# Where the weight sums of a seven-product feed-forward layer are made: VectorE or accumulating transfers

## The chip, the cores and the metric

The kernel runs on one core of a Trainium2 chip. The metric is device time in microseconds (us) of one execution. The engines are TensorE (PE, with its weight loads as PEld), VectorE (DVE), ScalarE (ACT), GpSimd (POOL) and SyncE (SP), whose queue issues most DMAs. Each engine works through its instructions in the order of the program and waits on semaphores.

## The reference

Two layers of a hybrid decoder over 16 + 512 tokens of width 1024: a norm, an input projection, two groups of attention heads, an output projection, then the feed-forward part with which the change deals (inner width 2816), and at the end a norm.

```python
hn = rmsnorm(h, ffn_norm_g)
ff = silu(einsum('bld,df->blf', hn, w_gate)) * einsum('bld,df->blf', hn, w_up)
return h + einsum('blf,fd->bld', ff, w_down)
```

## The kernel before

**Numbers.** Every product of two float32 matrices is three passes of TensorE in a rounded format (fp32r): high part of the weight by high part of the activation, high by low, low by high. A weight block is loaded to a tile (`raw` or `fraw`), ACT casts it to the high part (`whi`, `fwhi`, line 941) and DVE subtracts to get the low part (`wlo`, `fwlo`, line 942); both lines are in `splits`. `whi` and `fwhi` are rings of a few buffers, which come free when PE has used them.

**The feed-forward part.** The 2816 inner columns are 22 blocks of 128. Blocks 0 and 1 go plainly (`dense_steps`). Blocks 2 to 21 are objects of the class `Unit`: gate and up of a block together are treated as a 2 x 2 matrix of blocks (rows: gate and up; columns: the lower and the upper four of the eight 128-row pieces of the 1024 inputs), the tokens and inputs as another, and seven products of blocks take the place of eight. With a0, a1 the halves of gate and b0, b1 those of up, the seven products need the weights

- w1 = (a0, a1), the gate block as loaded (`make1`);
- w2 = (b0 + b1 - a0, b0 + b1), two sums that DVE makes into a tile `S` (lines 1084 and 1085, `make2`);
- w3 = (a0 - b0, b1), with one sum, made over b0 in `fraw` (line 1092, `make3`);
- w4 = a1 - (b0 + b1 - a0), made over a1 in `raw` (line 1098, `make4`).

The matching sums of activations are made once a layer in `x_forms` (four calls, k = 0 to 3): DVE makes four forms into `S`, and ACT and DVE split them into the tiles `th` and `tl` (line 155 is in `split`). `head` does the products of w1, `middle` those of w2 and the first half of w3, `tail` the rest. The seven products go into three PSUM banks, x, y and z. Bank x is accumulated on further and further, and between two accumulations ACT copies it out to a tile `e` (`keep`, line 1117), because its value so far is needed too; PE's next products into the same bank wait for that copy. At the end `done` makes silu(gate) times up and splits it into `ah` and `al`, the activations of the down products.

**Order.** `ffn` builds a list of steps, each a chunk of matmuls, and runs them in turn. Weights are jobs: `need(j)` at the first chunk of a job loads and converts the next few jobs ahead, so that loads (SP) and casts (ACT, DVE) stand well ahead of their products. Units 2 and 3 do their heads first, and then each unit's middle and tail are mixed with products of a round of down weights (`ROUNDS`, lines 27 to 30), whose blocks of w_down come into `raw` too. `raw` has four buffers, `fraw` and `S` two. GpSimd does nothing in the feed-forward part.

Of the kernel before, what the change touches and what calls it, by code (L numbers as in the profile page):

```python
# [16 lines left out]
NK = D // 128  # L17
# [24 lines left out]
def hybrid_kernel(ctx, tc, x_t, w_in, w_fl, w_out, w_gate, w_up, w_down, vecs, b_fg, rope, decay, mask, ident, out_t):  # L42
# [107 lines left out]
    def vcol(c):  # L150
        return vec[:, c:c + 1]
# [137 lines left out]
    def fft(tag, dt=F32R, shape=(128, T), bufs=None):  # L289
        return phase["ffn"].tile(list(shape), dt, name=tag, tag=tag, bufs=bufs)  # L290
# [570 lines left out]
    def ffn(l, st, real, last):  # L861
# [43 lines left out]
        def x_forms(k):  # L905
            def go():
                if k == 0:
                    st["t"] = [[fft(f"t{p}{i}", shape=(128, 2, 4, w)) for p in "hl"] for i in range(2)]
                s = fft("S", F32, (128, 6, w), 2)
                a, b = ((h[k][:, c0:c1], h[HB + k][:, c0:c1]) for c0, c1 in HC)  # L910
                g0, g1 = vcol(V_FFN + l * NK + k), vcol(V_FFN + l * NK + HB + k)
                with tc.issue_after(st["scaled"].ins) if real else ExitStack():
                    nc.scalar.activation(s[:, 0:2], two(h[k]), AF.Copy, scale=g0)
                nc.vector.tensor_sub(s[:, 2], s[:, 1], s[:, 0])
                for i in range(2):
                    nc.vector.scalar_tensor_tensor(s[:, 3 + i], b[1], g1, s[:, 1 + i], ALU.mult, ALU.subtract)
                nc.vector.scalar_tensor_tensor(s[:, 5], a[1], g1, s[:, 4], ALU.mult, ALU.subtract)
# [74 lines left out]
        class Pair:  # L992
# [14 lines left out]

            def make1(self, hi, lo):
                r = self.t["r"]
                s = self.t["s"] = fft("S", F32, (128, HB, 128), 2)  # L1010
# [33 lines left out]
            def steps(self):  # L1044
# [7 lines left out]
                        product(self.w2, 4, b(1, 1), y, False, True, 2, self.add(0, None, "zy")),  # L1052
                        product(self.w2, 2, form(r, 4), x, False, True, 2, self.add(1, 0, "x")))

        class Unit:
            def __init__(self, f):
                self.f = f
# [9 lines left out]

            def load(self):
                if "a" not in self.t:
                    for n, src, pool, tag, bufs in (("a", w_gate, wp, "raw", 4), ("b", w_up, phase["ffn"], "fraw", 2)):  # L1070
                        self.t[n] = pool.tile([128, NK, 128], F32, name=tag, tag=tag, bufs=bufs)
                        nc.sync.dma_start(self.t[n], src[l, self.f])


            def make1(self, hi, lo):
# [2 lines left out]


            def make2(self, hi, lo):  # L1080
                a, b = self.t["a"], self.t["b"]
                s = self.t["s"] = fft("S", F32, (128, NK, 128), 2)
                with tc.high_priority() if self.f == PLAIN else ExitStack():
                    nc.vector.tensor_add(s[:, HB:NK], b[:, 0:HB], b[:, HB:NK])
                    nc.vector.tensor_sub(s[:, 0:HB], s[:, HB:NK], a[:, 0:HB])
                    splits(hi, lo, s)


            def make3(self, hi, lo):
                a, b = self.t["a"], self.t["b"]  # L1090
                with tc.high_priority(60) if self.f == PLAIN else ExitStack():
                    nc.vector.tensor_sub(b[:, 0:HB], a[:, 0:HB], b[:, 0:HB])
                    splits(hi, lo, b)


            def make4(self, hi, lo):
                a, s = self.t["a"], self.t["s"]
                nc.vector.tensor_sub(a[:, HB:NK], a[:, HB:NK], s[:, 0:HB])
                splits(hi, lo, a[:, HB:NK])

            def bank(self, n):
                def go():
# [24 lines left out]
            def done(self):  # L1127
                e = self.t["e"]
                sg = tt("sg")
                with tc.high_priority():  # L1130
                    nc.vector.tensor_add(two(sg), self.t["zy"][:, :, 0:w], e[:, 0:2])
                c = slice(t0, T)
                nc.vector.scalar_tensor_tensor(sg[:, c], sg[:, c], RSC, st["R"][:, c], ALU.mult, ALU.mult)
                silu(sg[:, c], None if self.f < NF - 1 else ROOTS if last else LOGS)
                u = tt("tq")
                nc.vector.scalar_tensor_tensor(u[:, c], sg[:, c], RSC, st["R"][:, c], ALU.mult, ALU.mult)
                u2 = two(u)
                nc.vector.tensor_mul(u2[:, 0], self.t["x"][:, 0:w], u2[:, 0])
                nc.vector.tensor_mul(u2[:, 1], e[:, 2], u2[:, 1])
# [74 lines left out]
        for r, (f0, f1) in enumerate(ROUNDS):  # L1214
            for f in range(f0, f1):
                if f < PLAIN:
                    if f == 0:
                        st["first"] = range(len(jobs), len(jobs) + 3)
                    steps += dense_steps(w_gate[l, f], [(0, xs, NK, QC, g_done(f) if f else held.append)], banks=f == 1, own=own, far=f == 1, after=st["after"][2 * f])
                    steps += dense_steps(w_up[l, f], [(0, xs, NK, QC, u_done(f))], own=None if f else own, far=f == 0, after=st["after"][1 + 2 * f])  # L1220
                    continue
                for i in (f, f + 1) if f == PLAIN else (f,):
                    if i not in units:
                        units[i] = Unit(i)
                        steps += units[i].head()
# [32 lines left out]
        else:  # L1258
# [46 lines left out]

            def square_b(m):
                if m == 0:
                    t = fft("S", F32, (128, 6, w), 2)
# [89 lines left out]
            def after_7():  # L1398
# [23 lines left out]
        return steps  # L1422

    gf = const.tile([128, NK], F32, name="gf")
    nc.vector.tensor_scalar_mul(gf, vec[:, V_FIN:V_FIN + NK], RSC)

# [200 lines left out]
```

## Time and profile before

| what | us |
|---|---|
| time, median of 3 runs | 1249.9 (1249.72 to 1250.13) |
| span of the profiled execution | 1248.2 |
| TensorE busy | 1236.6 (99%) |
| VectorE busy | 1062.2 (85%) |
| ScalarE busy | 733.5 (59%) |
| GpSimd busy | 294.6 (24%) |
| the two feed-forward parts, about | 270 to 655 and 890 to 1190 |

The profiled execution's time is its span of 1248.2 us, 1.7 us under the median of the runs. A row of a group of instructions reads: line, engine, operation, tiles written and read, shape, count, then busy us and mean ns of one, then the idle time of the engine just before them and what ended it. A row of a stretch reads: from and to, its length, then busy us of PE, PEld, DVE, ACT and POOL (with the number of instructions), the clock granted to TensorE, the mean share of the time in which the 16 DMA engines were busy, and GB/s. A row of a timeline reads: start, length, and the instruction, with the wait ahead of it in brackets. A DMA row ends with the size and the median us from issue to landing. Times up to about 655 are the first layer.

### The profile page before, as it was taken

The page shows a single profiled execution, that of the slowest core. Times are in us where ns is not written, and L with a number is a line of the kernel's source. Part 1 is how long each engine was busy: PE and PEld are TensorE (multiplying, and loading weights), DVE is VectorE, ACT ScalarE, POOL GpSimd, SP SyncE. Part 2 cuts the span into 40 slices and gives each one's busy share as a digit, 9 for nine tenths or more (in the row PEclk, how much of TensorE's full clock was granted, in tenths as well). Part 3 has the DMA queues.
Part 4 walks back from the last instruction along what each step waited for, and adds up shares of the span by engine and source line. Part 5 has one row for each costly group of instructions (what it writes and reads, how often), then busy time and mean ns, then how long its engine had stood idle before and what let it go on. Part 6 is the DMA issues. An engine that isn't in the chain of part 4 may idle for free.

```text
span 1248.2 us, 24164 instructions
## 1 busy us (share of the span) xinstructions
PE 1236.6 (99%) x9387; PEld 1192.1 (96%) x9387; DVE 1062.2 (85%) x2033; ACT 733.5 (59%) x1397; POOL 294.6 (24%) x568
## 2 busy tenths in 40 slices
PE   9999999999999999999999999999999999999997
PEld 9999999999999999999999989999799999999996
DVE  7887756889997999899876877568999989998996
ACT  7767655776544555455566766567765445454554
POOL 4555655440000000000035556554400000000000
PEclk9999999999999999999999999999999999999999
DMA  6222222222433233322312222231414333333322
GB/s 238 68 77 69 78 69 85 60 85 72 133 119 102 85 102 118 103 86 85 114 65 85 63 84 75 68 94 52 141 54 135 111 102 102 100 104 102 102 69 69
DMA packets 43347, 116.25 MB, mean 93 GB/s; under 512 B 5088, under 2 KB 9952, under 8 KB 43232
## 3 DMA queue, kind: packets, MB, share of 16 engines
q1 hardware_dynamic: 42800, 114.41, 28.8%
q8 instruction: 74, 1.21, 0.4%
q14 instruction: 41, 0.34, 0.1%
q10 hardware_dynamic: 432, 0.29, 0.1%
HBM read 112.58 MB, written 2.10 MB: 92 GB/s over the span
## 4 chain that ended last, share of the span: by engine, by line
PE 90%; DVE 5%; ACT 2%; DMA 1%; issue 1%; SPq 0%; ACTq 0%; DVEq 0%
PE psd L231 28%; PE psa L953 22%; PE psd L953 15%; PE psd L1197 8%; PE psa L231 5%; PE psa L1197 3%; PE psa L452 2%; PE psa L619 2%; PE psa L549 1%; PE psa L753 1%; PE psa L789 1%; DMA raw<-w_down 1%; DVE wlo L942 1%; DVE fwlo L942 0%; PE psa L312 0%
## 5 line engine op out<-in xcount | busy, mean ns | idle before, releaser
L208 POOL TENSOR_TENSOR wlo<-raw,whi 128x128 fp32r<-128x128 f32 x488 | 254.6, 557 | 212.2 <-ACT whi L204 212.2
L231 PE MATMUL psd<-xh,whi 128*128 128x264 f32 (+1 forms) x696 | 169.7, 313 | 0.0
L231 PE MATMUL psd<-xh,wlo 128*128 128x264 f32 (+1 forms) x696 | 161.0, 301 | 0.0
L231 PE MATMUL psd<-xl,whi 128*128 128x264 f32 (+1 forms) x696 | 160.6, 300 | 0.0
L231 PEld LDWEIGHTS psd<-xh,whi 128*128 128x128 f32 x696 | 112.6, 190 | 3.3 <-ACT whi L204 0.3
L231 PEld LDWEIGHTS psd<-xh,wlo 128*128 128x128 f32 x696 | 111.1, 188 | 4.4
L231 PEld LDWEIGHTS psd<-xl,whi 128*128 128x128 f32 x696 | 111.7, 189 | 2.5
L941 ACT CAST fwhi<-raw 128x512 fp32r<-128x512 f32 (+2 forms) x88 | 66.2, 757 | 72.3 <-PE psd L953 28.7
L204 ACT CAST whi<-raw 128x512 fp32r<-128x512 f32 (+1 forms) x140 | 82.1, 612 | 32.5 <-PE psd L231 17.3
L127 POOL MEMSET kc<- 64x528 f32 x4 | 2.1, 534 | 367.5 <-PE psd L1197 367.3
L942 DVE TENSOR_TENSOR fwlo<-raw,fwhi 128x512 fp32r<-128x512 f32 (+2 forms) x88 | 75.1, 854 | 7.5 <-ACT fwhi L941 7.4
L941 ACT CAST whi<-raw 128x1024 fp32r<-128x1024 f32 (+2 forms) x72 | 56.8, 789 | 37.6 <-PE psd L953 21.1
L1117 ACT COPY e<-psa 128x264 f32<-128x264 f32 (+1 forms) x120 | 44.9, 374 | 53.5 <-PE psa L953 51.9
L953 PE MATMUL psa<-th,fwhi 128*128 128x264 f32 (+1 forms) x248 | 70.4, 284 | 0.0
L953 PE MATMUL psa<-tl,fwhi 128*128 128x264 f32 (+1 forms) x248 | 70.1, 283 | 0.0
L953 PE MATMUL psa<-th,fwlo 128*128 128x264 f32 (+1 forms) x248 | 70.1, 283 | 0.0
L953 PE MATMUL psa<-th,whi 128*128 128x264 f32 (+1 forms) x232 | 65.4, 282 | 0.0
L942 DVE TENSOR_TENSOR wlo<-raw,whi 128x1024 fp32r<-128x1024 f32 (+1 forms) x72 | 64.1, 893 | 1.5 <-ACT whi L941 1.4
L953 PE MATMUL psa<-tl,whi 128*128 128x264 f32 (+1 forms) x232 | 65.4, 282 | 0.0
L953 PE MATMUL psa<-th,wlo 128*128 128x264 f32 (+1 forms) x232 | 65.3, 281 | 0.0
L566 ACT ACTIVATE pr<-pr,nmax 128x144 f32<-128x144 f32 (+1 forms) x64 | 36.8, 575 | 45.7 <-DVE nmax L553 26.3
L941 ACT CAST fwhi<-S 128x1024 fp32r<-128x1024 f32 (+1 forms) x34 | 28.8, 846 | 34.0 <-PE psa L953 14.3
(442 smaller groups left out, 4381.7 us busy)
## 6 DMA issues: line engine op xcount, KB each, us to landing
raw<-w_in SPq DMA_DIRECT2D x54, 512.0 KB, 3.5
raw<-w_gate SPq DMA_DIRECT2D x44, 512.0 KB, 3.5
fraw<-w_up SPq DMA_DIRECT2D x40, 512.0 KB, 3.5
raw<-w_down SPq DMA_DIRECT2D x80, 256.0 KB, 3.7
raw<-w_out SPq DMA_DIRECT2D x16, 512.0 KB, 3.5
h<-x_t SPq DMA_DIRECT2D x8, 264.0 KB, 4.5
dec<-decay SPq DMA_DIRECT2D x8, 264.0 KB, 2.7
raw<-w_up SPq DMA_DIRECT2D x4, 512.0 KB, 3.9
```

Of the source, the lines that this page charges most:

```text
L204: pin(nc.scalar.copy(hi, job["raw"][:, c0:c1]), pinned)
L208: pin(sub(lo[:, c:c + step], job["raw"][:, c0 + c:c0 + c + step], hi[:, c:c + step].bitcast(F32)), pinned)
L231: nc.tensor.matmul(ps[1][b][:, 0:c1 - c0], w[:, wk, :], x[:, c0:c1], start=(k == 0 and i == 0), stop=(k == n - 1 and i == 2))
L452: nc.tensor.transpose(ps[:, 128 * j:128 * j + 128], src[:, o:o + 128], idt)
L549: nc.tensor.matmul(sc[0:nq, 0:c1 - c0], qq[:, q0:q0 + nq], kk[:, c0:c1], start=(i == 0), stop=(i == 1))
L566: nc.scalar.activation(pr, pr, AF.Exp, bias=nmax[0:nq], scale=-1.0, accum_out=rsum)
L619: nc.tensor.matmul(po[:, c0:SEQ], v[:, j, :], pp[:, j, META + c0:T], start=(j == 0 and i == 0), stop=(j == 4))
L941: nc.scalar.copy(hi, src)
L942: nc.vector.tensor_sub(lo, src, hi.bitcast(F32))
L953: nc.tensor.matmul(bank()[:, 0:b.shape[-1]], a[:, o + k, :], b, start=(fresh and k == 0 and i == 0), stop=(k == n - 1 and i == 2), skip_gr ...
L1117: nc.scalar.copy(self.t["e"][:, i], self.t["x"][:, 0:w])
L1197: nc.tensor.matmul(v[:, 0:c1 - c0], a[:, s * n + k, :], b[:, c0:c1], start=(k == 0 and i == 0), stop=(k == n - 1 and i == 2))
```

## The change

The sums are no longer made by DVE. A tile `F` of five quarter blocks a unit, F0 to F4 (128 x 5 x 4 x 128, two buffers), is loaded by SP and added to by DMAs that GpSimd issues with an add as they write:

1. SP loads up into F2 and F3 (b0, b1), and gate quarters into F1 (a0), F0 (a0 again) and F4 (a1).
2. GpSimd adds up from memory into F1 and F2 (accumulate 1): F1 = a0 + b0 there, and F2 = b0 + b1. Where a difference was needed a sum stands, and the signs of the tokens' forms are turned to match. The order of the five quarters gives w2 as F0 and F2, w3 as F1 and F3, and w4 as F4.
3. GpSimd adds F2 into F0 (accumulate 2), then F0 into F4 (accumulate 3).

The sums have no subtraction any more, so `x_forms` makes its forms with other signs (a constant `neg` with the negated norm weights, two small DVE instructions at the start, and -RSC in `done`), keeps them in activation tiles not yet in use instead of `S`, and splits each four forms in two halves. `raw` is still loaded with the whole gate block for w1. `fraw` is gone, `S` has one smaller buffer. `load_sums(f)` issues the loads and additions of unit f: two calls are put at fixed steps early in the list, and later ones stand ahead of the unit before the one that they serve.

```diff
+        def load_sums(f):
+            def go():
+                if f >= NF:
+                    return
+                t = wsum[f] = fft("F", F32, (128, 5, HB, 128), 2)
+                a, b = w_gate[l, f], w_up[l, f]
+                nc.sync.dma_start(t[:, 2:4], quarters(b))
+                for i, k in ((1, 0), (0, 0), (4, HB)):
+                    nc.sync.dma_start(t[:, i], a[:, k:k + HB])
+                nc.gpsimd.dma_start(t[:, 1:3], quarters(b), accum_op=ALU.add)
+                nc.gpsimd.dma_start(t[:, 0], t[:, 2], accum_op=ALU.add)
+                nc.gpsimd.dma_start(t[:, 4], t[:, 0], accum_op=ALU.add)
+            return go
...
             def make2(self, hi, lo):
-                a, b = self.t["a"], self.t["b"]
-                s = self.t["s"] = fft("S", F32, (128, NK, 128), 2)
                 with tc.high_priority() if self.f == PLAIN else ExitStack():
-                    nc.vector.tensor_add(s[:, HB:NK], b[:, 0:HB], b[:, HB:NK])
-                    nc.vector.tensor_sub(s[:, 0:HB], s[:, HB:NK], a[:, 0:HB])
-                    splits(hi, lo, s)
+                    splits(quarters(hi), quarters(lo), wsum[self.f][:, 0:3:2])
...
             def make3(self, hi, lo):
-                a, b = self.t["a"], self.t["b"]
                 with tc.high_priority(60) if self.f == PLAIN else ExitStack():
-                    nc.vector.tensor_sub(b[:, 0:HB], a[:, 0:HB], b[:, 0:HB])
-                    splits(hi, lo, b)
+                    splits(quarters(hi), quarters(lo), wsum[self.f][:, 1:4:2])
...
             def make4(self, hi, lo):
-                a, s = self.t["a"], self.t["s"]
-                nc.vector.tensor_sub(a[:, HB:NK], a[:, HB:NK], s[:, 0:HB])
-                splits(hi, lo, a[:, HB:NK])
+                splits(hi, lo, wsum.pop(self.f)[:, 4])
...
+                if f > PLAIN:
+                    steps.append(load_sums(f + 1))
...
+        steps.insert(20, load_sums(PLAIN + 1))
         for i in range(HB):
             steps.insert(NK + 4 + 7 * i, x_forms(i))
+        steps.insert(NK + 2, load_sums(PLAIN))
```

In `x_forms`, the lines that make and split the forms:

```diff
-                s = fft("S", F32, (128, 6, w), 2)
+                i = 3 * (k % 2)
+                s, o, e = (two(fft(f"a{'hl'[k // 2]}{2 + i + n}").bitcast(F32)) for n in range(3))
...
-                split(th, tl, s[:, 2:6])
+                split(th[:, 0:2], tl[:, 0:2], o)
+                split(th[:, 2:4], tl[:, 2:4], e)
```

The order of the instructions moves on three engines. On GpSimd, at the end of the first layer's attention part, this stood before (`wlo`-like splits of weights, then memsets for the second layer):

```order
L208 TENSOR_TENSOR kx_3887<-raw,kx_3886 128x128 x4
L208 TENSOR_TENSOR rql<-raw,rqh 128x128 x4
L208 TENSOR_TENSOR rkl<-raw,rkh 128x128 x4
L127 MEMSET kc_8550 64x528
L96 MEMSET qo_8548 64x528
```

Now the accumulating DMAs of the units stand between (line 1071 is accumulate 1, 1072 accumulate 2, 1073 accumulate 3):

```order
L208 TENSOR_TENSOR rql<-raw,rqh 128x128 x4
L208 TENSOR_TENSOR rkl<-raw,rkh 128x128 x4
L1071 DMA F<-w_up 128x1024
L1072 DMA F<-F 128x512
L1071 DMA F<-w_up 128x1024
L1073 DMA F<-F 128x512
L1072 DMA F<-F 128x512
L1073 DMA F<-F 128x512
L1071 DMA F<-w_up 128x1024
L1072 DMA F<-F 128x512
```

Sixty of them a layer, three a unit, are in GpSimd's queue, where there was nothing between the attention part and the memsets of the next layer.

On ACT, around the w2 cast of unit 6 in the first layer (`S_5127` before), with the copies of unit 5's bank x (`e_5023`):

```order
L941 CAST fwhi_5070<-raw_4924 128x512
L1117 COPY e_5023<-psa_5010 128x264
L441 ACTIVATE sg_4979<-sg_4979 128x528
L941 CAST fwhi_5125<-S_5127 128x1024
L1117 COPY e_5023<-psa_5010 128x264
L155 CAST ah4_4987<-tq_4983 128x528
L941 CAST whi_5093<-raw_5089 128x1024
L1117 COPY e_5023<-psa_5010 128x264
```

The same place now (`F_5030` is unit 6's tile, `F_4864` unit 5's, `e_5055` unit 5's copies):

```order
L943 CAST fwhi_5102<-F_4864 128x512
L441 ACTIVATE sg_5004<-sg_5004 128x528
L1129 COPY e_5055<-psa_5042 128x264
L943 CAST fwhi_5154<-F_5030 128x1024
L155 CAST ah4_5012<-tq_5008 128x528
L1129 COPY e_5055<-psa_5042 128x264
L943 CAST whi_5122<-raw_5120 128x1024
L1129 COPY e_5055<-psa_5042 128x264
```

The w2 cast stands ahead of the second copy as before, but reads a tile that accumulates 1 and 2 fill, and the cast `ah4` has moved ahead of the copy.

On SP, before, the loads of units 6 and 7 with down weights between:

```order
L1072 DMA raw_5089<-w_gate 128x1024
L1072 DMA fraw_5091<-w_up 128x1024
L1177 DMA raw_5203<-w_down 128x512 x2
L1072 DMA fraw_5256<-w_up 128x1024
L1072 DMA raw_5254<-w_gate 128x1024
```

And now, with the loads of F for unit 6 behind the plain gate loads of units 6 and 7:

```order
L1092 DMA raw_5120<-w_gate 128x1024
L1189 DMA raw_5236<-w_down 128x512 x2
L1092 DMA raw_5286<-w_gate 128x1024
L1068 DMA F_5030<-w_up 128x1024
L1070 DMA F_5030<-w_gate 128x512 x3
L1189 DMA raw_5429<-w_down 128x512 x2
```

Each unit's two loads have become five, and those of F go behind the gate block of the next unit.

More of the change, by code (lines that the diff above doesn't have):

```diff
@@ L908, in go @@
                     st["t"] = [[fft(f"t{p}{i}", shape=(128, 2, 4, w)) for p in "hl"] for i in range(2)]
-                s = fft("S", F32, (128, 6, w), 2)
+                i = 3 * (k % 2)
+                s, o, e = (two(fft(f"a{'hl'[k // 2]}{2 + i + n}").bitcast(F32)) for n in range(3))
                 a, b = ((h[k][:, c0:c1], h[HB + k][:, c0:c1]) for c0, c1 in HC)
-                g0, g1 = vcol(V_FFN + l * NK + k), vcol(V_FFN + l * NK + HB + k)
+                g0, g1, g2 = vcol(V_FFN + l * NK + k), vcol(V_FFN + l * NK + HB + k), neg[:, l * HB + k:l * HB + k + 1]
                 with tc.issue_after(st["scaled"].ins) if real else ExitStack():
[L913 to L917, printed above, removed]
+                    nc.scalar.activation(s, two(h[k]), AF.Copy, scale=g0)
+                nc.vector.tensor_sub(o[:, 0], s[:, 0], s[:, 1])
+                nc.vector.scalar_tensor_tensor(o[:, 1], b[1], g1, s[:, 1], ALU.mult, ALU.subtract)
+                nc.vector.scalar_tensor_tensor(e[:, 0], b[1], g2, o[:, 0], ALU.mult, ALU.subtract)
+                nc.vector.scalar_tensor_tensor(e[:, 1], a[1], g2, e[:, 0], ALU.mult, ALU.subtract)
                 th, tl = (t[:, k % 2] for t in st["t"][k // 2])
-                split(th, tl, s[:, 2:6])
+                split(th[:, 0:2], tl[:, 0:2], o)
+                split(th[:, 2:4], tl[:, 2:4], e)
             return go
@@ L1009, in make1 @@
                 r = self.t["r"]
-                s = self.t["s"] = fft("S", F32, (128, HB, 128), 2)
+                s = self.t["s"] = fft("S", F32, (128, HB, 128), 1)
                 splits(hi[:, 0:4], lo[:, 0:4], r[:, 0:4])
@@ L1053, in steps, with quarters @@
                         product(self.w2, 2, form(r, 4), x, False, True, 2, self.add(1, 0, "x")))
+        wsum = {}
+        def quarters(t):
+            return t.rearrange("p (s k) c -> p s k c", s=2)
+        def load_sums(f):
[11 more added lines that the diff above has]
+            return go
         class Unit:
@@ L1069, in load @@
                 if "a" not in self.t:
-                    for n, src, pool, tag, bufs in (("a", w_gate, wp, "raw", 4), ("b", w_up, phase["ffn"], "fraw", 2)):
-                        self.t[n] = pool.tile([128, NK, 128], F32, name=tag, tag=tag, bufs=bufs)
-                        nc.sync.dma_start(self.t[n], src[l, self.f])
+                    self.t["a"] = wp.tile([128, NK, 128], F32, name="raw", tag="raw", bufs=4)
+                    nc.sync.dma_start(self.t["a"], w_gate[l, self.f])
             def make1(self, hi, lo):
@@ L1135, in done @@
                 u = tt("tq")
-                nc.vector.scalar_tensor_tensor(u[:, c], sg[:, c], RSC, st["R"][:, c], ALU.mult, ALU.mult)
+                nc.vector.scalar_tensor_tensor(u[:, c], sg[:, c], -RSC, st["R"][:, c], ALU.mult, ALU.mult)
                 u2 = two(u)
@@ L1307, in square_b @@
                 if m == 0:
-                    t = fft("S", F32, (128, 6, w), 2)
+                    t = fft("F", F32, (128, 6, w), 2)
                     fin["one"] = [t[:, i, 0:nb] for i in range(3)]
@@ L1422, in ffn @@
         return steps
+    neg = const.tile([128, DEPTH * HB], F32, name="neg")
+    for i in range(DEPTH):
+        nc.vector.tensor_scalar_mul(neg[:, i * HB:i * HB + HB], vec[:, V_FFN + i * NK + HB:V_FFN + i * NK + NK], -1.0)
     gf = const.tile([128, NK], F32, name="gf")
```

## The prediction

> **What bounds the kernel now.** I read the page first (busy time by engine, then the chain that ended last), then the stretches by stage, then what TensorE waited for.
>
> ```profile
> span 1248.2 us, 24164 instructions
> PE 1236.6 (99%) x9387; PEld 1192.1 (96%) x9387; DVE 1062.2 (85%) x2033; ACT 733.5 (59%) x1397; POOL 294.6 (24%) x568
> PE 90%; DVE 5%; ACT 2%; DMA 1%; issue 1%; SPq 0%; ACTq 0%; DVEq 0%
> ```
>
> TensorE (PE) is busy for 1236.6 of 1248.2 us, so all engines together can give back at most 11.6 us while its matmuls stay as they are; the change leaves their number alone. The stretches (length, then busy PE, PEld, DVE, ACT, POOL, granted clock, DMA share, GB/s) say where those 11.6 us lie:
>
> ```profile
> 340.00:425.00 85.00, 85.00 (x700) 85.00 (x699) 76.17 (x128) 40.77 (x63) 0.00 (x0) 1.00 0.32 98
> 425.00:485.00 60.00, 60.00 (x495) 60.00 (x494) 59.66 (x108) 32.44 (x52) 0.00 (x0) 1.00 0.31 102
> 600.00:634.00 34.00, 33.53 (x270) 32.72 (x268) 27.84 (x44) 18.77 (x28) 0.00 (x0) 1.00 0.39 130
> 1190.00:1248.00 58.00, 49.71 (x411) 48.77 (x409) 46.54 (x93) 29.95 (x60) 0.00 (x0) 0.96 0.23 74
> ```
>
> 8.3 us are in the last stretch, the final norm and output, where no unit is left. From 425 to 485 VectorE (DVE) is busy for 59.66 of 60 us and PE still never stops; its pace, 60.00/495 = 0.121 us a matmul, is that of the stretch before (85.00/700 = 0.121), where DVE has 9 us to spare. A full DVE does not slow PE here. PE's waits by name (total, times, longest):
>
> ```profile
> PE psa L1458 <- DVE wide L64: 1.6, 1, 1.6
> PE psd L953 <- DVE al L155: 0.3, 1, 0.3
> PE psd L1197 <- DVE al L155: 0.2, 1, 0.2
> PE psd L1197 <- ACT ah L155: 0.2, 1, 0.2
> PE psd L953 <- ACT ah L155: 0.2, 1, 0.2
> ```
>
> Lines 953 and 1197 are the feed-forward products: 0.3 + 0.2 + 0.2 + 0.2 = **0.9 us** of waits, all on splits of activations. That is all the change can win there.
>
> **What it removes.** The four sums of each of the 40 units:
>
> ```profile
> L1092 DVE TENSOR_TENSOR fraw<-raw,fraw 128x512 f32<-128x512 f32 x40 | 27.3, 684 | 0.0
> L1085 DVE TENSOR_TENSOR S<-S,raw 128x512 f32<-128x512 f32 x40 | 27.3, 684 | 0.2 <-DMA raw<-w_gate 0.2
> L1098 DVE TENSOR_TENSOR raw<-raw,S 128x512 f32<-128x512 f32 x40 | 27.3, 683 | 0.0
> L1084 DVE TENSOR_TENSOR S<-fraw 128x512 f32<-128x512 f32 x40 | 27.0, 684 | 0.3 <-DMA fraw<-w_up 0.3
> ```
>
> 27.3 + 27.3 + 27.3 + 27.0 = 108.9 us come off DVE, beside PE work: 0 on the end, at best the 0.9 us above.
>
> **What it adds to DVE and ScalarE (ACT).** In x_forms each split of 1056 columns becomes two of 528, eight times:
>
> ```profile
> L155 DVE TENSOR_TENSOR tl<-S,th 128x1056 fp32r<-128x1056 f32 x4 | 5.0, 1249 | 0.0
> L155 DVE TENSOR_TENSOR al<-tq,ah 128x528 fp32r<-128x528 f32 x18 | 12.6, 702 | 0.8 <-ACT ah L155 0.7
> L155 ACT CAST th<-S 128x1056 fp32r<-128x1056 f32 x4 | 4.3, 1078 | 4.4 <-DVE S L917 4.3
> L155 ACT CAST ah<-tq 128x528 fp32r<-128x528 f32 x18 | 11.4, 634 | 11.5 <-DVE tq L1139 10.7 <-DVE tq L896 0.9
> ```
>
> DVE: 8 x (2 x 702 - 1249) = 1.2 us; ACT: 8 x (2 x 634 - 1078) = 1.5 us. Both lie under products of the first two blocks; without that cover they cost at most 2.7 us, with it 0. The two constants of signs, the sign of RSC and the smaller tile S change no duration that ends late: 0.
>
> **What it moves.** The sums become a chain that no engine computes: a slot of tile F comes free; SP loads up (512 KB) and three quarters of gate (256 KB); GpSimd adds up to two quarters (accumulate 1), then one quarter to another (accumulate 2), then a third (accumulate 3). Its price, from the table of DMA issues (count, KB each, median us to landing) and the rate row of 281 to 290 us:
>
> ```profile
> raw<-w_gate SPq DMA_DIRECT2D x44, 512.0 KB, 3.5
> raw<-w_down SPq DMA_DIRECT2D x16, 128.0 KB, 2.8
> GB/s 73 0 0 0 0 91 237 36 36 146 400 309 437 419 401 437 400 473 400 346 219 237 309 400 400 419 255 164 164 178 219 269 159 132 46 18 0 73 155 287
> ```
>
> At about 420 GB/s 512 KB take 1.25 us to move, so a load is 2.25 fixed + 1.25. The up load with the first gate quarter behind it lands after 2.25 + 1.25 + 0.62 = 4.1 us. No accumulating transfer is in this trace, so I bound it. Low end: the price of a plain load, 3.5 and (2.25 + 0.62 =) 2.9, chain C = 4.1 + 3.5 + 2.9 = 10.5. High end: a read and a write-back in turn, two plain loads each, 7.0 + 5.8, and 1.1 for GpSimd's own work (below): C = 18.0. I take the moving part twice, since an addition has two operands to fetch, with the fixed part once: 2.25 + 2 x 1.25 = 4.75 and 2.25 + 2 x 0.62 = 3.5; and for GpSimd's work on the two issues 2 x 0.56 us, the nearest thing it does, a small instruction:
>
> ```profile
> L208 POOL TENSOR_TENSOR wlo<-raw,whi 128x128 fp32r<-128x128 f32 x488 | 254.6, 557 | 212.2 <-ACT whi L204 212.2
> ```
>
> And the weight loads go on beside it: the stretch from 340 to 425 has a DMA share of 0.32, so over its whole length the chain shares the engines for about a third of the time, 0.32 x 1.25 = 0.4 us for a load met on the way. **C = 4.1 + 4.75 + 3.5 + 1.1 + 0.4 = 13.9 us.** That is near the middle of the two ends; the fixed part, which is most of the load's row, is in both. A rule that speaks against the change: the Trainium skill, "Collectives: The Full Stack", section "The bandwidth ceiling", has a reduction in the transfer engines at half a copy's rate, since the add needs two source reads. By it the two transfers would be 4.75 and 3.5, by plain copies 3.5 and 2.9; no run here shows either.
>
> **Where it would wait.** ACT runs in order. The cast of accumulate 2's result (weights w2 of unit f) stands ahead of the copy e that empties a bank of unit f-1, and PE's next products go into that bank. Unit 6 in layer 0 (start, length, then what, on ACT, DVE and PE):
>
> ```profile
> 335.77 0.68 DVE L942 TENSOR_TENSOR wlo<-raw,whi 128x512 fp32r<-128x512 f32 x1
> 348.03 1.05 ACT L941 CAST fwhi<-S 128x1024 fp32r<-128x1024 f32 x1 [0.41 <-PE psd L953]
> 349.62 0.38 ACT L1117 COPY e<-psa 128x264 f32<-128x264 f32 x1 [0.53 <-PE psa L953]
> 349.89 0.64 ACT L155 CAST ah<-tq 128x528 fp32r<-128x528 f32 x1
> ```
>
> The first row is the last reading of unit 4's w4, after which F's slot is free: 336.4. PE writes the bank again at 350.87 (below), so the copy may start at 350.4; with cast ah now between them the w2 cast may start at 350.4 - 0.55 - 1.05 = 348.8. Allowed: **12.4 us**. The other places by the distance between the same two PE instants, w1 of f-2 done and the bank's next products:
>
> ```profile
> 308.26 0.28 PE L953 MATMUL psa<-xh,fwhi 128*128 128x264 f32 x1
> 324.57 0.28 PE L953 MATMUL psa<-th,fwhi 128*128 128x264 f32 x1
> ...
> 334.79 0.28 PE L953 MATMUL psa<-th,fwhi 128*128 128x264 f32 x1
> 350.87 0.28 PE L953 MATMUL psa<-th,fwhi 128*128 128x264 f32 x1
> ...
> 361.09 0.28 PE L953 MATMUL psa<-th,fwhi 128*128 128x264 f32 x1
> 380.11 0.28 PE L953 MATMUL psa<-th,fwhi 128*128 128x264 f32 x1
> ...
> 923.73 0.28 PE L953 MATMUL psa<-xh,fwhi 128*128 128x256 f32 x1
> 939.35 0.29 PE L953 MATMUL psa<-th,fwhi 128*128 128x256 f32 x1
> ...
> 949.27 0.28 PE L953 MATMUL psa<-th,fwhi 128*128 128x256 f32 x1
> 964.77 0.29 PE L953 MATMUL psa<-th,fwhi 128*128 128x256 f32 x1
> ```
>
> Unit 6's 16.1 us leave 12.4, so 3.7 go to the cast, split and copies. Unit 4 in layer 0: 16.3, allowed 12.6; units 4 and 6 in layer 1: 15.6 and 15.5, allowed 11.9 and 11.8. For unit 8 more down products lie between and the distance is 19.0, allowed 15.3; units 8 and 16 of both layers have that, the rest more. With C = 13.9 the four tight places cost 1.3 + 1.5 + 2.0 + 2.1 = **6.9 us**, less the 0.9 won: +6.0, a span of 1254.2. The profiled span of before is 1.7 below the runs' median of 1249.9, so **1255.9**. The ends: C = 10.5 costs nothing, 1249.0; C = 18.0 costs 5.4 + 5.6 + 6.1 + 6.2 + 4 x 2.7 - 0.9 = +33, 1283.
>
> SP issues five loads a unit where it issued two; behind them in its queue stand down weights, which go ahead of their use into one of four slots: 0, at most the 1.25 us of a load once a place. The bytes rise by 0.75 MB of loads and 1 MB of additions a unit, per 13 us about 135 GB/s on top of the 98 above; beside the 400 GB/s and more that the rate row reaches, the engines keep up, or the chain loses what B below charges. GpSimd has nothing else to do in these stretches (POOL 0.00 above), and its accumulates for a unit stand in the order of the loads; the first units' stand behind nothing that waits for them.
>
> **The rivals.** (A) *In time.* If an accumulating transfer costs about a plain load and GpSimd's part is hidden, C stays under 13.0: 1249.0 where it is below 11.8, up to 1252.3 at 13.0, no change (0.2%, 2.5 us, is about what a measurement of this kernel can tell from no change). For it: the fixed part dominates the rows; against: two transfers and a load in series leave 12 us little room. It decides at C = 13.0, where the four add up to 0.4 + 0.6 + 1.1 + 1.2 = 3.3 us, 2.4 after the 0.9. (C = 11.6, both additions at a plain load's price with 1.1 for GpSimd, is its likeliest: 1249.0.) (B) *Starved issues.* GpSimd's preparation of a transfer is held up by DVE, which is busy for 76.17 of 85 us around units 6 to 10: if each of the two issues waits out two DVE instructions (2 x 1.2 us by the row of 1249 ns), C = 18.7, 6.1 + 6.3 + 6.8 + 6.9 + 4 x 3.4 - 0.9 = +39 us, 1289; half of that, C = 16.3, gives 3.7 + 3.9 + 4.4 + 4.5 + 4 x 1.0 - 0.9 = +20, 1269. For it: DVE's share; against: no row shows the two meeting. The Trainium skill, "SBUF — State Buffer", section "Who interferes with whom", states such a lock for DVE's two-port instructions and not for tensor_tensor, which most here are; no run here shows it. (C) *A relieved DVE frees PE.* All of PE's waits on DVE in these products are 0.5 us, so even with ACT's it is 1249.0, not faster by 0.2%; to be faster, PE's pace itself would have to rise, against the equal paces above. That the sums are not taken off DVE is excluded by the program, which has no such instruction left.
>
> **How the numbers follow.** The chain late at the tight places (C from 13.0 to 15): 0.42, and the likeliest, 1255.9; its own range, +2.4 at 13.0 to 2.4 + 2.6 + 3.1 + 3.2 - 0.9 = +10.4 at 15, is 1252.3 to 1260.3. In time: 0.38. Starved or twice as dear (C over 15): 0.16. Faster by over 0.2%: 0.04. So faster 0.04, same 0.38, slower 0.58. The range runs from A's 1249.0 less the runs' spread, 1248.7, to C = 17 (4.4 + 4.6 + 5.1 + 5.2 + 4 x 1.7 - 0.9 = +25), 1275.
>
> **What would show it.** In the profile after: DVE near 1062.2 - 108.9 + 1.2 = 954.5 busy us; accumulates landing 4 to 6 us after issue; PE waits on line 955's products for the copy e, and ACT's w2 cast ended by a DMA rather than by PE, at units 4 and 6. If PE shows no such waits, A holds; if units 8 and 16 show them too, B; if waits lie elsewhere, at w4 or at a layer's first units, my reading of the order is wrong.

## The result, and the profile after

The changed kernel takes 1330.4 us (1325.7 to 1337.4, 4 runs) against 1250.0 us before (1249.7 to 1250.3): ratio 1.0646, 95% interval 1.0614 to 1.0678. The forecast was 1255.9 and its range ended at 1275, so the direction was right and the size was far off. The profiled execution has a span of 1323.9 us, 75.7 us more than the 1248.2 of before. The page's totals, the two DMA queues that matter (packets, MB, share of the 16 engines' span) and the issues:

```profile
span 1323.9 us, 24633 instructions
PE 1256.6 (95%) x9387; PEld 1208.2 (91%) x9387; DVE 979.4 (74%) x1883; ACT 733.3 (55%) x1405; POOL 399.7 (30%) x688
q1 hardware_dynamic: 60080, 145.88, 34.4%
q0 software_dynamic: 17280, 41.95, 18.4%
F<-w_up POOLq DMA_DIRECT2D x40, 512.0 KB, 6.4
F<-F POOLq DMA_DIRECT2D x80, 256.0 KB, 4.6
```

PE's idle time rose from 11.6 to 1323.9 - 1256.6 = 67.3 us, 55.7 more, and its busy time by 20.0 us for the same 9387 matmuls. The waits of PE say where the first part is (total, times, longest):

```profile
PE psa L955 <- ACT e L1129: 46.9, 8, 9.6
PE psa L955 <- DVE fwlo L944: 4.9, 1, 4.9
PE psa L955 <- DVE h L1043: 3.4, 3, 1.8
```

The first row is the wait that the prediction named, at eight places: units 4, 6, 8 and 16 of both layers. The stretches around two of them show the second part, in the column behind the instruction counts (the granted clock) and the next (the DMA share):

```profile
316.00:340.00 24.00, 16.12 (x113) 15.91 (x112) 11.55 (x20) 6.80 (x12) 3.50 (x4) 0.79 0.80 215
340.00:425.00 85.00, 77.74 (x622) 77.32 (x622) 53.51 (x84) 35.36 (x54) 13.10 (x15) 0.96 0.79 198
425.00:485.00 60.00, 59.48 (x490) 59.26 (x489) 53.18 (x98) 30.75 (x53) 9.60 (x11) 1.00 0.78 196
```

From 340 to 425 the clock was 1.00 and the DMA share 0.32 before. Now the share is 0.79, and the clock is below 1.00 in the two stretches that hold a long stall. Unit 6 of the first layer, the place that the prediction worked through, on SP, GpSimd, ACT and PE (one fence an engine, start, length, operation, the wait ahead of it):

```profile
348.74 0.33 SPq L1068 DMA_DIRECT2D F<-w_up  x1
349.12 1.37 SPq L1070 DMA_DIRECT2D F<-w_gate  x3
...
359.45 0.33 SPq L1068 DMA_DIRECT2D F<-w_up  x1
359.82 1.39 SPq L1070 DMA_DIRECT2D F<-w_gate  x3
```

```profile
353.95 0.88 POOL L1071 DMA_DIRECT2D F<-w_up  x1 [8.70 <-DVE h L1214]
359.74 0.86 POOL L1072 DMA_DIRECT2D F<-F  x1 [4.91 <-DMA F<-w_up]
367.76 0.86 POOL L1073 DMA_DIRECT2D F<-F  x1 [7.16 <-DMA F<-F]
```

```profile
367.52 1.04 ACT L943 CAST fwhi<-F 128x1024 fp32r<-128x1024 f32 x1 [8.37 <-DMA F<-w_gate]
368.47 0.63 ACT L155 CAST ah<-tq 128x528 fp32r<-128x528 f32 x1
369.01 0.37 ACT L1129 COPY e<-psa 128x264 f32<-128x264 f32 x1
```

```profile
369.43 0.59 PE L955 MATMUL psa<-th,fwhi 128*128 128x264 f32 x1 [6.55 <-ACT e L1129]
369.82 0.42 PE L955 MATMUL psa<-tl,fwhi 128*128 128x264 f32 x1
```

SP issues the loads at 348.7; accumulate 1 is issued 5.2 us later, accumulate 2 another 5.8 later, and ACT's cast starts 7.8 later: a chain of 18.8 us where 13.9 were forecast. ACT has stood for 8.4 us in front of the copy, and PE for 6.55. The releaser that the cast's row names (a load) is not the last one: the cast reads what accumulate 2 writes, and at unit 6 of the second layer and at both units 16 the profile names accumulates (F<-F) ahead of the same cast. The last step of the chain is the longest: at 359.45, just before accumulate 2 is issued, SP starts the next unit's four loads of 1.25 MB. The other places show the same pattern: at the units 4 the next unit's loads start together with accumulate 1, and that step is the long one (7.9 and 9.7 us); at the units 16 they start 1.8 and 1.4 us ahead of accumulate 2, which takes 8.0 and 7.8 us; at the units 8 they start 1.6 to 1.7 us behind it, it takes 5.1 us, and PE waits only 0.7 and 1.1 us.

### The profile page after: what moved, and what is told of

It is laid out like the page before. It is cut to its first block, busy times and chain, and to the rows that moved or that the text cites. A ratio compares the mean times of both kernels' runs of the same rounds, so it can differ in the third digit from the quotient of the medians.

```text
span 1323.9 us, 24633 instructions
## 1 busy us (share of the span) xinstructions
PE 1256.6 (95%) x9387; PEld 1208.2 (91%) x9387; DVE 979.4 (74%) x1883; ACT 733.3 (55%) x1405; POOL 399.7 (30%) x688
## 3 DMA queue, kind: packets, MB, share of 16 engines
q0 software_dynamic: 17280, 41.95, 18.4%
## 4 chain that ended last, share of the span: by engine, by line
PE 69%; DVE 10%; DMA 9%; issue 7%; ACT 4%; POOL 0%; SPq 0%; DVEq 0%; ACTq 0%; POOLq 0%
PE psd L231 22%; PE psa L955 17%; PE psd L955 11%; PE psd L1209 6%; DMA F<-F 4%; PE psa L231 3%; DMA F<-w_gate 2%; PE psa L1209 2%; PE psa L452 2%; PE psa L619 2%; PE psa L549 1%; PE psa L753 1%; DMA F<-w_up 1%; PE psa L789 1%; DVE wlo L944 1%
## 5 line engine op out<-in xcount | busy, mean ns | idle before, releaser
L943 ACT CAST fwhi<-F 128x1024 fp32r<-128x1024 f32 (+1 forms) x62 | 55.6, 896 | 128.4 <-DMA F<-F 54.4
L944 DVE TENSOR_TENSOR fwlo<-F,fwhi 128x1024 fp32r<-128x1024 f32 (+1 forms) x62 | 63.9, 1032 | 79.2 <-ACT fwhi L943 78.9
L955 PE MATMUL psa<-th,fwhi 128*128 128x264 f32 (+1 forms) x248 | 74.6, 301 | 47.0 <-ACT e L1129 46.9
L1072 POOL DMA_DIRECT2D F<-F x40 | 34.8, 869 | 230.1 <-DMA F<-w_up 222.9
L204 ACT CAST whi<-raw 128x512 fp32r<-128x512 f32 (+1 forms) x140 | 82.3, 612 | 31.9 <-PE psd L231 17.3
L1071 POOL DMA_DIRECT2D F<-w_up x40 | 37.4, 934 | 205.9 <-DMA F<-w_gate 103.0
L955 PEld LDWEIGHTS psa<-th,fwhi 128*128 128x128 f32 x248 | 49.9, 201 | 49.0 <-ACT e L1129 48.8
L943 ACT CAST whi<-F 128x1024 fp32r<-128x1024 f32 (+1 forms) x58 | 53.1, 916 | 68.6 <-PE psa L955 37.1
L943 ACT CAST fwhi<-raw 128x1024 fp32r<-128x1024 f32 (+2 forms) x66 | 51.9, 801 | 60.5 <-PE psa L955 29.6
L1073 POOL DMA_DIRECT2D F<-F x40 | 34.7, 868 | 163.4 <-DMA F<-F 157.9
L944 DVE TENSOR_TENSOR wlo<-F,whi 128x1024 fp32r<-128x1024 f32 (+1 forms) x58 | 61.2, 1055 | 19.5 <-ACT whi L943 19.0
L944 DVE TENSOR_TENSOR fwlo<-raw,fwhi 128x1024 fp32r<-128x1024 f32 (+2 forms) x66 | 60.3, 914 | 18.8 <-ACT fwhi L943 17.3
```

The source lines that it names most:

```text
L204: pin(nc.scalar.copy(hi, job["raw"][:, c0:c1]), pinned)
L943: nc.scalar.copy(hi, src)
L944: nc.vector.tensor_sub(lo, src, hi.bitcast(F32))
L955: nc.tensor.matmul(bank()[:, 0:b.shape[-1]], a[:, o + k, :], b, start=(fresh and k == 0 and i == 0), stop=(k == n - 1 and i == 2), skip_gr ...
L1071: nc.gpsimd.dma_start(t[:, 1:3], quarters(b), accum_op=ALU.add)
L1072: nc.gpsimd.dma_start(t[:, 0], t[:, 2], accum_op=ALU.add)
```

## The experiments

The first theory: PE stalls because ACT stands, in order, at the cast of w2 in front of the copy, and the chain is long because its transfers share the DMA engines with the next unit's loads. The rivals: the loads alone, or the rest of the change, cost the time; accumulating transfers are that slow by themselves; the DMA engines are the bound whoever waits.

**No accumulating transfers.** The three lines with `accum_op` are taken out, so the sums are missing from the weights.

> Leaves out the three accumulating transfers of each unit, so the sums are missing from the weights; every load stays. Theory (the chain of load, accumulate 1, accumulate 2 is later than the ACT copy can bear): the chain ends with the loads, about 5 us after the slot is free instead of 18 to 20, under the 12 allowed, so the eight waits of PE on the copy e (46.9 us) go and the clock stays whole: 1249 to 1255. Rival 'loads alone' (0.75 MB more a unit and five issues on SP fill the queues): the waits stay in good part, above 1290.

Measured: 1248.9 us, ratio 0.9991 (0.9982 to 1.0000). No wait of PE on a copy e is left. The loads into F, the split forms, the signs and the order of the casts cost nothing that can be measured, and DVE's relief (978.9 us busy) gains about 1 us, as forecast, at the edge of what the interval can tell from nothing.

**DVE sums in F.** The same loads, but:

```diff
-                nc.gpsimd.dma_start(t[:, 1:3], quarters(b), accum_op=ALU.add)
-                nc.gpsimd.dma_start(t[:, 0], t[:, 2], accum_op=ALU.add)
-                nc.gpsimd.dma_start(t[:, 4], t[:, 0], accum_op=ALU.add)
...
+                    nc.vector.tensor_add(t[:, 1], t[:, 1], t[:, 2])
+                    nc.vector.tensor_add(t[:, 2], t[:, 2], t[:, 3])
+                    nc.vector.tensor_add(t[:, 0], t[:, 0], t[:, 2])
+                    nc.vector.tensor_add(t[:, 4], t[:, 4], t[:, 0])
                     splits(quarters(hi), quarters(lo), wsum[self.f][:, 0:3:2])
```

> The same loads into F, but DVE makes the sums in place (four additions of 128x512 a unit) and GpSimd issues nothing. Theory: the chain is the loads, about 5 us, and 2 x 0.7 us, under 12: no wait on the copy, 1249 to 1255, with DVE back at about 1062 to 1088 busy us; the changed forms of the activations and signs cost nothing. Rival 'the rest of the change costs' (order of ACT's casts, split forms, loads): above 1290.

Measured: 1263.3 us, ratio 1.0100 (1.0085 to 1.0115), 8 us above what was expected. PE's waits on the copy are down to 1.4 us in all; one other is there:

```profile
PE psa L955 <- DVE fwlo L944: 5.4, 1, 5.4
PE psa L955 <- ACT e L1131: 1.4, 3, 1.0
```

The first row stands at the start of the second layer's units, where DVE splits a w1 behind a run of forms of the activations. The changed kernel has that wait too (4.9 us); why it comes was not tried further. It is not the cause of the 75.7 us.

**w2's cast behind the copies.**

```diff
-                        nc.scalar.copy(self.t["e"][:, i], self.t["x"][:, 0:w])
+                        st["kept"] = nc.scalar.copy(self.t["e"][:, i], self.t["x"][:, 0:w]).ins
...
-                with tc.high_priority() if self.f == PLAIN else ExitStack():
+                with tc.high_priority() if self.f == PLAIN else tc.issue_after(st["kept"]) if self.f > PLAIN + 1 else ExitStack():
                     splits(quarters(hi), quarters(lo), wsum[self.f][:, 0:3:2])
```

> All transfers and sums as in the changed kernel, only ACT's cast of w2 is queued behind the copies e of the unit before. Theory (what stalls PE is ACT blocked in order ahead of the copy, not the weights themselves): at unit 6 PE first uses w2 some 24 us after the slot is free and the chain takes 18 to 20, so the waits on the copy go or shrink to a few us in all: 1250 to 1265. Rival 'the weights come too late for PE however they are queued' or 'the transfers' traffic is the bound': 1310 to 1335, with PE waiting on w2's low part instead.

Measured: 1285.5 us, ratio 1.0266 (1.0244 to 1.0289): more than half of the loss is gone by moving one split a unit in the queues, and PE's waits on the copy fall from 46.9 to 1.5 us, so ACT's order was what stalled PE there; but 20 us more stay than expected. The wait moved to DVE, in good part. PE waited 11.1 us in all for sg, which empties the other two banks; PE's waits, then DVE at the first such place:

```profile
PE psd L955 <- DVE sg L1143: 11.1, 4, 4.8
PE psa L955 <- ACT e L1129: 1.5, 3, 1.0
```

```profile
335.06 1.23 DVE L944 TENSOR_TENSOR fwlo<-F,fwhi 128x1024 fp32r<-128x1024 f32 x1 [5.87 <-ACT fwhi L943]
336.21 0.68 DVE L944 TENSOR_TENSOR fwlo<-raw,fwhi 128x512 fp32r<-128x512 f32 x1
336.81 0.70 DVE L1143 TENSOR_TENSOR sg<-psd,e 128x528 f32<-128x528 f32 x1
```

The low part of w2 stands ahead of sg in DVE's queue, as the high part had stood ahead of the copy in ACT's.

**Both halves behind.** As before, and DVE's half is queued behind sg of the unit before; so that this exists when the split is written, w4's job calls one job less ahead:

```diff
+                        s.enter_context(tc.issue_after(st["kept"]))
+                        s.enter_context(tc.issue_after(st["left"]))
...
+                jobs[u.w4]["reach"] = 2
```

> As the run with w2's cast behind the copies, and DVE's half of w2's split is queued behind the emptying of the other two banks (the operation that starts sg) of the unit before. Theory (PE stalls because an engine that works in order stands at w2's split ahead of the work that frees a bank): the 11.1 us that PE waited for sg in that run go with their slow clock, about 2 us each; what is left is the start of layer 1 (5.7) and the waits for h (8.5): 1260 to 1275. Rival 'the transfers are the bound and the wait only moves on': it shows on other products and the time stays at 1280 to 1300.

Measured: 1285.5 us, ratio 1.0283 (1.0263 to 1.0304), no faster than the run before. The rival's prediction holds here, not mine. The waits for sg are gone and others have come:

```profile
PE psa L955 <- ACT e L1134: 14.1, 5, 4.3
PE psa L955 <- DVE fwlo L944: 4.8, 1, 4.8
```

ACT's cast of w2, now close to its use, has waited 7.7 us for an accumulate at this place and holds up the next copies, for which PE waits 4.3 us:

```profile
996.34 1.05 ACT L943 CAST fwhi<-F 128x1024 fp32r<-128x1024 f32 x1 [7.67 <-DMA F<-F]
```

A chain that is put off is late somewhere else.

**The next unit's loads held back.** In `load_sums`, each of the four loads waits until accumulate 2 of the unit before has landed (`quiet`), then the same for odd units only (`quiet2`, with `f % 2 and` in front of the condition: the tight places are at even units).

```diff
+                    if f - 1 in second:
+                        tc.add_manual_dep(load.ins, second[f - 1].name, mybir.DependencyInfo(
+                            mybir.DependencyClass.Sync, mybir.DependencyReason.DATA), reason="quiet")
```

> The loads of the next unit's F wait until accumulate 2 of the unit before has landed; all else as in the changed kernel. Theory (accumulate 2 is slowed from 3.4 to 5 to 8 us, and accumulate 1 from 5.9 to about 8, by the 1.25 MB of the next unit's loads beside it): the chain takes 5.0 + 5.9 + 3.4 = 14.2 us at the tight places, waits on the copy fall from 46.9 to about 14 us, 1270 to 1285. Rival 'an accumulating transfer is that dear by itself': accumulates keep 6 to 8 us and the time stays 1320 to 1340.

Measured: 1332.6 us, ratio 1.0653 (1.0629 to 1.0678), no faster. But the chain at unit 6 is what the theory says of it (SP, GpSimd, ACT):

```profile
348.90 0.33 SPq L1068 DMA_DIRECT2D F<-w_up  x1
```

```profile
354.86 0.88 POOL L1073 DMA_DIRECT2D F<-w_up  x1 [4.82 <-DVE wlo L944]
361.08 0.86 POOL L1074 DMA_DIRECT2D F<-F  x1 [5.34 <-DMA F<-w_up]
```

```profile
364.48 1.04 ACT L943 CAST fwhi<-F 128x1024 fp32r<-128x1024 f32 x1 [6.90 <-DMA F<-F]
```

6.0 + 6.2 + 3.4 = 15.6 us where it was 18.8, and accumulate 2 takes 3.4 where it took 7.8. The waits on the copy stayed at 46.1 us, over 13 places instead of 8. A reason that the profile shows is that the added wait made the loads themselves start late: unit 6's slot was free at 346.87 (the end of DVE's split of unit 4's w4), and its loads waited until 348.90 for unit 5's accumulate 2.

> Only the odd units' loads wait for accumulate 2 of the even unit before; the even units, where the tight places are, wait for their slot alone. Theory (the next unit's loads beside it make accumulate 2 of an even unit 8 us instead of 3.4): from the load's issue the chain takes 5.9 + 5.9 + 3.4 = 15.2 at even units, the waits on the copy fall from 46.9 to about 25 us and the slow clock behind them too: 1285 to 1305. Rival 'it is the accumulate itself': 1320 to 1335.

Measured: 1309.9 us, ratio 1.0483 (1.0465 to 1.0500), 20 us faster than the changed kernel but 5 us over the theory's range; the waits on the copy fell from 46.9 to 34.1 us, not to 25. So the next unit's loads are a part of it, and not the whole; the odd units' chains, late now, add small waits of their own (12 places in all).

**Copies in place of additions.** The three transfers without `accum_op`: same sizes, places and order, and the additions left out.

> The same three transfers by GpSimd, of the same sizes in the same order, but they overwrite and do not add: the additions are left out. Theory (an addition moves its bytes at about half the rate of a copy, and the rest is fixed cost and traffic): the 512 KB transfer lands in about 5 us instead of 6.4 and the chain is 2 to 4 us shorter at the eight tight places: 1285 to 1318, and the share of the DMA engines' time of that queue falls from 18 to about 10%. Rival 'the price is GpSimd's issue, not the addition': 1325 to 1337.

Measured: 1278.2 us, ratio 1.0230 (1.0213 to 1.0247), 7 us better than my lower end. The queue and the issues answer to the first rows of after:

```profile
q0 software_dynamic: 12160, 41.95, 9.2%
F<-w_up POOLq DMA_DIRECT2D x40, 512.0 KB, 4.3
F<-F POOLq DMA_DIRECT2D x80, 256.0 KB, 2.7
PE psa L955 <- ACT e L1129: 18.1, 5, 5.6
```

For the same 41.95 MB the engines are busy for 9.2% of 1276.1 = 117 us where the additions took 18.4% of 1323.9 = 244 us: 2.1 times. Each transfer lands about 2 us sooner. The addition, not GpSimd's issue, is the dear part. Still, 28 us of the loss stay: a chain of three plain copies is too late for ACT as well, at five places.

**Only w2 by DVE.** DVE makes F2 and F0; F1 and F4 stay accumulating transfers, 256 KB each, that do not stand on one another (F4's is issued by w4's job now).

> DVE makes the two sums of w2 in F again; w3's and w4's sums stay accumulating transfers, 256 KB each, one chain no longer standing on the other. Theory (the latency of the chain ahead of w2 is what stalls): w2 is ready about 5 to 7 us after the slot is free, under 12; no waits on the copy, at most those at the start of layer 1 (5 us and 2 of slow clock): 1249 to 1262. Rival 'accumulating transfers cost wherever they stand': about half the loss stays, 1285 to 1295.

Measured: 1261.4 us, ratio 1.0093 (1.0071 to 1.0115), at the upper end of the theory's range. One wait of 2.4 us on a copy is left, and 2.5 us at the start of layer 1. With the chain ahead of w2 gone, most of the loss is gone. The run also halves the bytes that are added (20.98 MB), so by itself it does not tell the chain from the time of the additions.

**A stall without any transfer.** The kernel before, with 20 more copies of the same bank on ACT ahead of the second copy of units 3, 5, 7 and 15:

```diff
+                        for _ in range(20 if i == 1 and self.f in (3, 5, 7, 15) else 0):
+                            nc.scalar.copy(self.t["e"][:, 2], self.t["x"][:, 0:w])
                         nc.scalar.copy(self.t["e"][:, i], self.t["x"][:, 0:w])
```

> The kernel before, with ACT held up ahead of the second copy e of units 3, 5, 7 and 15 of both layers by 20 extra copies of the same bank (20 x 0.27 to 0.38 us, less about 1 us of slack: PE waits 4.4 to 6.6 us at eight places, 35 to 53 us). No transfer is changed. Theory (a PE that has stood still for some us goes on at half clock for 4 to 5 us): 2 to 2.5 us more at each place, 1301 to 1323, granted clock about 0.98. Rival 'the slow clock comes with the traffic or with GpSimd': only the waits, 1285 to 1303, clock 0.998 as before.

Measured: 1336.4 us, ratio 1.0689 (1.0673 to 1.0705). The waits were longer than I worked out (67.8 us at eight places), so the sum of 1301 to 1323 was missed; what it was to tell apart is clear. PE is busy for 1253.9 us, 17.3 more than before, 2.2 us a place. The waits, and the stretches around the first stall:

```profile
PE psa L953 <- ACT e L1119: 67.8, 8, 9.3
```

```profile
324.00:328.00 4.00, 0.78 (x7) 0.57 (x5) 4.00 (x6) 3.87 (x10) 0.00 (x0) 1.00 0.24 68
...
332.00:336.00 4.00, 2.29 (x10) 2.29 (x11) 0.00 (x0) 1.57 (x5) 0.00 (x0) 0.50 0.00 0
336.00:340.00 4.00, 4.00 (x26) 4.00 (x25) 1.21 (x3) 0.38 (x1) 0.00 (x0) 0.70 0.01 4
340.00:344.00 4.00, 4.00 (x35) 4.00 (x34) 2.70 (x4) 2.52 (x3) 0.00 (x0) 1.00 0.27 96
```

The clock is 0.50 when PE goes on at 333.71, and whole again within some 5 us; the DMA share is 0.00 and 0.01 there, so it is no traffic. The slow clock comes from the standstill.

**The additions aside.** The same three accumulating transfers, one after the other, into two quarters of F that nobody reads; w2, w3 and w4 are cast from what was loaded, so the sums are left out.

```diff
-                nc.gpsimd.dma_start(t[:, 1:3], quarters(b), accum_op=ALU.add)
-                nc.gpsimd.dma_start(t[:, 0], t[:, 2], accum_op=ALU.add)
-                nc.gpsimd.dma_start(t[:, 4], t[:, 0], accum_op=ALU.add)
+                nc.gpsimd.dma_start(t[:, 3:5], quarters(b), accum_op=ALU.add)
+                nc.gpsimd.dma_start(t[:, 3], t[:, 2], accum_op=ALU.add)
+                nc.gpsimd.dma_start(t[:, 4], t[:, 3], accum_op=ALU.add)
```

> The same three accumulating transfers, of the same sizes from the same places and one after the other, but they add into two quarters of F that no engine reads (w2 is taken from F0 and F2 as loaded, w3 from F1 and F2, w4 from the gate block): the additions are left out of what is computed, the traffic stays. Theory (the loss is the wait of w2's split for the chain, ahead of the copy in ACT's queue): nothing waits, 1249 to 1258. Rival 'the DMA engines at 80 to 90% of their time are the bound themselves, whoever waits': loads come late everywhere and the time is 1275 to 1300.

Measured: 1276.0 us, ratio 1.0206 (1.0182 to 1.0230). The rival is right about a third of the loss: with no engine waiting for a sum, 26 us stay. GpSimd in this run, around units 6 and 7:

```profile
349.26 0.99 POOL L1071 DMA_DIRECT2D F<-w_up  x1
355.91 0.86 POOL L1072 DMA_DIRECT2D F<-F  x1 [5.66 <-DMA F<-w_up]
364.83 0.86 POOL L1073 DMA_DIRECT2D F<-F  x1 [8.06 <-DMA F<-F]
365.57 1.03 POOL L1071 DMA_DIRECT2D F<-w_up  x1
```

One unit's three additions take GpSimd from 349.26 to 365.57, 16.3 us, nearly all of it waiting, and the next begin at once. A unit takes PE 13 to 16 us. The slot comes free only behind the last addition, and on SP the other weights stand behind the loads that wait for the slot. SP's wait for accumulates ahead of the loads of F, then ACT behind such a late load:

```profile
SPq L1068 <- DMA F<-F: 263.6, 35, 14.8
```

```profile
361.40 1.05 ACT L943 CAST fwhi<-raw 128x1024 fp32r<-128x1024 f32 x1 [4.27 <-DMA raw<-w_gate]
...
363.30 0.37 ACT L1129 COPY e<-psa 128x264 f32<-128x264 f32 x1
```

Here it is the cast of a gate block that holds up the copy, and PE waits 1.7 us for it. So a part of these 26 us comes through ACT's order again: PE's waits on the copy are 10.1 us in this run.

**Copies aside.** The same program, word for word in its order, without the additions.

> As the run that adds into two quarters which no engine reads, in the same order on every engine, but the three transfers overwrite and do not add: no addition is made at all. Theory (what still cost 26 us there is the time of the additions themselves: GpSimd waits out three of them one after the other, 15 to 16 us a unit, as long as PE takes for a unit, so slots come free late and loads behind them on SP too): copies land 2 us sooner each, GpSimd's chain is 10 to 11 us a unit, the slots are free in time and it is 1249 to 1257. Rival 'it is the number of transfers or the order on SP': 1268 to 1280 again.

Measured: 1249.0 us, ratio 0.9990 (0.9980 to 0.9999). SP waits 43.4 us for transfers of F where it waited 263.6. So it is the time of the additions, and not the number of transfers, their bytes or SP's order.

No run with additions by transfer came closer to the kernel before than 11 us, and the two fastest runs, without any additions, stop at 1248.9 and 1249.0: PE has nothing more to give. A third buffer of F, which would start the chain a unit sooner, was not tried; it needs 10 KB a partition more.

## Why the prediction was wrong, step by step

- **What can be won** (0.9 us): right. The two fastest kernels without additions are 1.2 and 1.7 us under their own runs of before.
- **DVE's relief** (to 954.5 us busy): 979.4. Rows of back-to-back instructions overlap (one of 0.68 us starts 0.60 after another), so busy time falls by less than the sum of their rows: with the 160 sums back on DVE it was 1067.1, 87.7 more, and not 108.9. Nothing hangs on it.
- **The place**: right. Copy e, ACT in order, units 4 and 6 first, and units 8 and 16, which the prediction had waiting only with a longer chain.
- **The chain**: the step that failed. The prediction took 4.1 + 4.75 + 3.5 + 1.1 + 0.4 = 13.9 us. Measured at unit 6: 5.2 + 5.8 + 7.8 = 18.8, and 15.6 with the next unit's loads held back. The parts that the held-back chain has were 2 us too small: the load 6.0 where 4.1 stood, accumulate 1 with its issue 6.2 where 5.3 stood, accumulate 2 with its issue 3.4 where 4.1 stood. The term for traffic was 0.4 us where 18.8 - 15.6 = 3.2 were measured, and the sentence that the DMA engines "keep up" was wrong: I set 135 GB/s more against the 400 that a burst reaches. The right sum was in engine time: 0.32 of the engines' time went for 98 GB/s, so 0.75 MB of loads and 1 MB of additions at double price, some 2.75 MB in 13 us or 210 GB/s, need 0.69 more. That is a share near 1; 0.79 with the stalls was measured, and 0.85 in the run whose additions nobody waits for. GB/s do not show it: that run moves 219 (first row), and its twin with copies moves 232 at a share of 0.68 (second row) and loses nothing:

```profile
340.00:425.00 85.00, 79.48 (x644) 78.43 (x643) 57.18 (x92) 35.53 (x57) 13.18 (x15) 1.00 0.85 219
340.00:425.00 85.00, 85.00 (x701) 85.00 (x701) 64.25 (x105) 40.04 (x62) 9.67 (x18) 1.00 0.68 232
```

- **What is allowed** (12.4 us): right at unit 6. The chain less PE's wait is 18.8 - 6.55 = 12.2 us. Over the eight places the figure was 0.8 us too large on average, and 2.5 us at unit 4 of the first layer (18.0 - 7.9 = 10.1 against 12.6).
- **The clock**: missing from the sum. 20.0 us of the 75.7 are matmuls at a lower clock behind stalls, and the run with stalls alone shows 2.2 us a place. The rest of the 75.7 us are PE's waits: 46.9 on the copy, 4.9 and 3.4 on two others. By the prediction's own sum C = 18.8 at all places would have cost 39.6 us.
- **The rivals.** A fell. B had the right distance (C = 18.7) and, as it said, waits at units 8 and 16 too, but the wrong mechanism. GpSimd issues each transfer in 0.9 us, and unit 4's accumulate 1 took 7.9 us, among the longest, in a stretch where DVE (third busy number) did little, 1.03 of the 4 us from 324, with a DMA share of 1.06:

```profile
321.29 0.86 POOL L1071 DMA_DIRECT2D F<-w_up  x1 [11.22 <-ACT fwhi L943]
329.17 0.88 POOL L1072 DMA_DIRECT2D F<-F  x1 [7.03 <-DMA F<-w_up]
```

```profile
324.00:328.00 4.00, 2.02 (x17) 1.80 (x15) 1.03 (x2) 0.06 (x1) 0.00 (x0) 1.00 1.06 273
```

  Its price, 1289, left out the clock as well. That the additions' own length holds up slots and loads, 26 us with nobody waiting for a sum, was in no rival.

Some things stay open: why PE waits about 5 us at the start of the second layer, and how the 80 us divide by cause, since the parts (ACT's order, traffic, the additions' length, the clock) are not independent.

## What to carry to other kernels

Work moved from an idle corner of a busy engine to a queue has a latency, and the engine that consumes it in order passes the whole wait on to what stands behind; look for the nearest thing behind it, not for its own use. Before adding transfers, turn the DMA share of the stage into a budget in engine time, with additions at twice the price, and add up what a unit of work will need. A standstill of TensorE costs more than its length.

## What the runs showed of the hardware

- An accumulating transfer keeps the DMA engines busy 2.1 times as long as a copy of the same bytes (244 against 117 us for 41.95 MB) and lands about 2 us later (512 KB 6.4 against 4.3, 256 KB 4.6 against 2.7). The Trainium skill, "Collectives: The Full Stack", section "The bandwidth ceiling", which the prediction named, states half a copy's rate for the reduction of a collective; the factor measured here is close to that.
- After each of the eight waits of 8.0 to 9.3 us in the run with stalls alone TensorE went on at a granted clock of 0.50, for 3 to 5 us, 2.2 us lost each time on average. In all the runs the same followed every wait of 2.3 us and more in the feed-forward parts, some of those from 1.7 to 1.9 us, and none up to 1.5 us. The Trainium skill, "TensorE: Matmul & The Clock Gate", section "Part 1: The HAM clock gate", puts the idle window at about 3.4 us; here shorter waits, from 1.8 to 3.0 us, cost clock too.
- An accumulate of 256 KB takes longer beside other loads: at unit 6 accumulate 2 took 3.4 us with the next unit's loads held back and 7.8 us beside these 1.25 MB.
